# Attention scores of one layer as products over 64 rows, one softmax map on each half of the TensorE array

## The chip, the cores and the metric

The kernel runs on one core of a Trainium2 chip. The metric is the device time of one execution in microseconds (us). The kernel before takes 610.21 us, the median of three runs (609.72 to 611.18).

The engines are called by the profile's short names: PE is TensorE's matmul, PEld the loading of its stationary operand, DVE is VectorE, ACT is ScalarE, POOL is GpSimd, and SP is the engine that issues most of the DMAs. PSUM is the memory that PE writes, in banks of 128 partitions by 512 numbers.

## The reference

One decoder layer on 512 tokens of width 1024, in float32. One projection makes nine groups of columns. Branch A is a gated MLP over chunks of 128 tokens; branch B is differential attention with 8 heads; both are projected, gated, merged and projected again, and a LayerNorm ends the layer. What the change touches is the scores of branch B:

```python
q = apply_rope(qh.reshape(bn, s_len, B_HEADS, 2, B_QK_DIM), cos, sin) * (B_QK_DIM ** -0.5)
k = apply_rope(kh.reshape(bn, s_len, B_HEADS, 2, B_QK_DIM), cos, sin)
...
sc = jnp.einsum("bqhmd,bkhmd->bhmqk", qblk, k, preferred_element_type=jnp.float32)
sc = jnp.where(mask, sc, -jnp.inf)
pr = jax.nn.softmax(sc, axis=-1)
a = pr[:, :, 0] - lam * pr[:, :, 1]
return jnp.einsum("bhqk,bkhd->bqhd", a.astype(v.dtype), v)
```

Each of the 8 heads has two softmax maps (m = 0 and 1), and each map has queries and keys of 64 numbers (`B_QK_DIM`, in the kernel `DK`). The queries are taken 128 at a time, so a head has four blocks, and block i looks at (i + 1) * 128 keys: 128, 256, 384 or 512.

## The kernel before

**Products.** PE multiplies a stationary operand (128 rows by 128 columns, loaded first) with a moving one (128 rows by up to 512 columns); the sum runs over the rows, that is over SBUF's partitions. The operands are of the type float32r, which keeps fewer bits than float32. So a float32 number is kept as two parts, high (its rounding to float32r) and low (the rest), and a product is made of several. For the large projections `three` (line 279) makes three: high by high, high by low, low by high.

**Order of the work.** The whole program is one list of instructions in a written order. `product` (line 267) issues a product of the projections and counts it. `later(n, fn)` (line 262) puts a piece of other work on an agenda, to be issued n products later. So the attention runs between the products of other projections: `attention` (line 871) gives each of the 32 blocks (8 heads by 4) a starting count, some 13 to 23 products apart (`PERIOD`, for the last two heads times 0.78). At a block's start `scores` is issued, 10 to 13 products later `combine`, at the start of the block two further on `transposes`, and one further on `values`. Only the products of `product` are counted: those of the scores, the transposes and the values are not, so the agenda does not move when their number changes.

**Rotary and stacks.** `rope` (line 694) handles a pair of heads (p = 0 to 3) for q or k. Two feature groups of the projection come out as two banks, A with the first half of the rotated numbers and B with the second. DVE makes the rotated halves (`turn`, `join`), ACT rounds them to their high parts (`high`, line 707), POOL subtracts to get the low parts (`low`, line 712). The four planes are kept in one tile `hl`, 128 partitions by 4 planes by 512 tokens, in the order high of half 0, high of half 1, low of half 1, low of half 0. A partition of `hl` is one of 32 frequencies times four (two heads by two maps).

`get` (line 720), 14 or 18 products after `low`, then makes the **stacks** with DMAs on SP's queue: for each head and map the 32 partitions by 4 planes are laid out as 128 partitions. A stack tile is 128 partitions by 2 maps by 512 tokens. So all 128 rows of one map's product carry the 64 numbers twice, as high and as low parts. For k there is a second stack `kx` with the planes in reversed order, so that its high parts lie opposite the low parts of q. For the first pair (p = 0) `kx` is made much later from `k` by `change_over` (line 735, 290 products on, `SWAP`), with four DMAs of 32 partitions for each head, because the buffers that `kx` has (the tag "kx") hold sums of weights at first (line 941).

**Scores.** `scores` (line 763) makes, for one block of one head, two products for each map: q by k (high by high and low by low, in one sum over 128 rows) and q by kx (high by low and low by high). Each map writes its own PSUM bank (`ps_sc`, two buffers). DVE then adds the mask and takes the smallest value (line 776), and ACT takes the exponential (line 782).

Of the kernel before, what the change touches and what calls it, by code (L numbers as in the profile page):

```python
# [13 lines left out]
F32 = mybir.dt.float32  # L14
F32R = mybir.dt.float32r
BF16 = mybir.dt.bfloat16
I32 = mybir.dt.int32
AF = mybir.ActivationFunctionType
# [3 lines left out]
P = 128  # L22
D = 1024
T = 512
# [3 lines left out]
DK = 64  # L28
# [15 lines left out]
ROPE_Q = (2, 6, 8, 20, 22)  # L44
STACK = (14, 4)
FIRST_STACK = (20, 4)
SWAP = 290
BEGIN = 14
STRETCH = 0.78
PERIOD = (13, 16, 20, 23)  # L50
# [183 lines left out]
def hybrid_layer(ctx: ExitStack, tc: tile.TileContext, a, out: bass.AP):  # L234
    nc = tc.nc
    pe, dve, act, pool, sp = nc.tensor, nc.vector, nc.scalar, nc.gpsimd, nc.sync
# [9 lines left out]
    def pbank(tag, bufs):  # L246
        return psum.tile([P, T], F32, tag=tag, name=f"ps_{tag}", bufs=bufs)

    def pp():
        return pbank("pp", 3)  # L250
# [11 lines left out]
    def later(n, fn, *args):  # L262

        clock[1] += 1
        heapq.heappush(agenda, (clock[0] + n, clock[1], fn, args))
# [132 lines left out]
    def next_unit(name):  # L398
        u = cursor[0]
        assert STEPS[u][0] == name, (STEPS[u][0], name)  # L400
        cursor[0] += 1
        for g in (prep(u), prep(u + 1), prep(u + 2)):
            run(g)
        if not pumping:
            for v in range(u + 3, u + 6):
                run(load(v))
        spread(u + 3)
        if name in EARLY_ASK:
            later(ASK, lambda: run(load(u + 6)))
        return split.pop(u)  # L410
# [31 lines left out]
    def feature_group(ps, name, mh, ml):  # L442
        h, l = next_unit(name)
        for k in range(KT):
            s = slice(k * P, (k + 1) * P)
            three(ps, h[:, s], l[:, s], mh[:, k, :], ml[:, k, :], k == 0, k == KT - 1)
# [36 lines left out]
    ap_ = attn.enter_context(tc.tile_pool(name="attn", bufs=1))  # L483
# [23 lines left out]
    def small(shape, name, bufs=6):  # L507
        return consts.tile(shape, F32, name=name, tag=name, bufs=bufs)
# [183 lines left out]
    stacks = {}  # L692

    def rope(name, p, banks=None, at=None, stack=STACK):

        A, B = banks or (pp(), pp())
        m, parts = [], []

        def turn(bank, table):
            m.append(rp.tile([P, T], F32, name="m", tag="m", bufs=6))  # L700
            dve.tensor_tensor(out=m[-1], in0=bank, in1=table, op=OP.mult)

        def join():
            dve.tensor_tensor(out=m[0], in0=m[0], in1=m[3], op=OP.subtract)
            dve.tensor_tensor(out=m[2], in0=m[2], in1=m[1], op=OP.add)

        def high():
            parts.append(rp.tile([P, 4, T], F32R, name="hl", tag="hl"))
            for j in range(2):
                act.activation(parts[0][:, j, :], m[2 * j], AF.Copy)  # L710

        def low():
            hl = parts[0]
            for j in range(2):
                pool.tensor_tensor(out=hl[:, 3 - j, :], in0=m[2 * j], in1=hl[:, j, :].bitcast(F32),  # L715
                                   op=OP.subtract)
            for hd in range(2):
                later(stack[0] + stack[1] * hd, get, hd)

        def get(hd):  # L720


            h = 2 * p + hd
            for n in ("k", "kx") if name == "k" and p else (name,):
                s = ap_.tile([P, 2, T], F32R, name=n, tag=n, bufs=3)
                stacks[n, h] = s
                for i in range(2):
                    rows = parts[0][2 * hd + i:P:4]
                    if n == "kx":
                        rows = rows[:, ::-1]  # L730
                    sp.dma_start(out=s[:, i, :].bitcast(F32), in_=rows.bitcast(F32))
            if name == "k" and p == 0:
                later(SWAP + 6 * hd, change_over, h)

        def change_over(h):
            s = ap_.tile([P, 2, T], F32R, name="kx", tag="kx", bufs=3)
            stacks["kx", h] = s
            for b in range(4):
                sp.dma_start(out=s[b:P:4].bitcast(F32), in_=stacks["k", h][3 - b:P:4].bitcast(F32))

        at = at or ROPE[:2] + (ROPE if name == "k" else ROPE_Q)
        for i, bank in enumerate((A, B)):
            if not banks:
                feature_group(bank, name, xh, xl)
            later(at[2 * i], turn, bank, cs)
            later(at[2 * i + 1], turn, bank, sn)
        for n, fn in zip(at[4:], (join, high, low)):
            later(n, fn)
# [13 lines left out]

    def scores(h, i):
        n = (i + 1) * P
        q, k0, k1 = stacks["q", h], stacks["k", h], stacks["kx", h]
        sc = [pbank("sc", 2) for _ in range(2)]
        for m in range(2):
            for o, kk in enumerate((k0, k1)):
                pe.matmul(sc[m][:, :n], q[:, m, i * P:(i + 1) * P], kk[:, m, :n],  # L769
                          start=o == 0, stop=o == 1)  # L770
        pr = [ap_.tile([P, T], F32, name=f"p{m}", tag=f"p{m}", bufs=3) for m in range(2)]
        if i == 0:
            todo["st", h] = small([P, NT, 4], "sth", 2)
        st = todo["st", h][:, i, :]
        for m in range(2):
            dve.tensor_tensor_reduce(out=pr[m][:, :n], in0=sc[m][:, :n], in1=mask[:, T - n:],  # L776
                                     scale=-(DK ** -0.5), scalar=3e38, op0=OP.add, op1=OP.min,
                                     accum_out=st[:, m:m + 1])
            if m == 0:
                dve.tensor_scalar(out=st[:, 0:1], in0=st[:, 0:1], scalar1=-math.log(T),  # L780
                                  scalar2=None, op0=OP.add)
            act.activation(pr[m][:, :n], pr[m][:, :n], AF.Exp, bias=st[:, m:m + 1], scale=-1.0,  # L782
                           accum_out=st[:, 2 + m:3 + m])
        todo[h, i] = pr, st
# [75 lines left out]
    def block(h, i, starts):  # L860
        e = NT * h + i
        later(starts[e], scores, h, i)
        later(starts[e] + COMBINE[i], combine, h, i)
        later(starts[e + 2], transposes, h, i)
        later(starts[e + 3], values, h, i)
        if i == NT - 1:
            tail = TAIL if h < 5 else LAST_TAIL
            for d, fn in zip(tail, (squares, norm, scale, gated)):
                later(starts[e + 3] + d, fn, h)
# [76 lines left out]
    for k in range(KT):  # L946
        if k % 2 == 0:
            h, l = next_unit("kq")
        s = [slice((k % 2) * T + i * P, (k % 2) * T + (i + 1) * P) for i in range(4)]
# [6 lines left out]
        else:  # L956
            for i, bank in enumerate(first_kq):
                three(bank, h[:, s[i]], l[:, s[i]], xh[:, k, :], xl[:, k, :], False, k == KT - 1)
    rope("k", 0, first_kq[:2], TURN_K, FIRST_STACK)
    rope("q", 0, first_kq[2:], TURN_Q, STACK)  # L960
    first_ua = ua_pair(0, (pbank("tr", 1), pbank("po", 1)))

# [23 lines left out]
    for p in range(1, 4):  # L986
        rope("k", p)
        rope("q", p)
        later(GATE, ua_pair(p, (pp(), pp())))
# [273 lines left out]
    for c in (1, 0):  # L1263
        h, l = next_unit("ple")
        for t in range(NT):
            ts = slice(t * P, (t + 1) * P)
            for k in range(2):
                m = slice(k * T, (k + 1) * T)
# [103 lines left out]
    for those in ((0, 1), (2, 3)):  # L1372
        for k in range(KT):
# [9 lines left out]
            h, l = units[k // 2]  # L1383
            m = slice((k % 2) * T, (k % 2 + 1) * T)
# [9 lines left out]
    for t in range(NT):  # L1394
        ts = slice(t * P, (t + 1) * P)
        for i, (c0, c1) in enumerate(last_columns[t][1:], 1):
            for k in range(KT):
# [4 lines left out]
                h, l = units[k // 2]  # L1402
                m = slice((k % 2) * T + c0 - T, (k % 2) * T + c1 - T)
# [45 lines left out]
```

## Time and profile before

| What | Value |
|---|---|
| median of three runs | 610.21 us |
| the profiled execution, its own time | 610.13 us |
| its span, first to last instruction | 608.2 us |
| PE busy | 600.1 us (99%), 2880 products |
| weight loads (PEld) | 503.1 us (83%) |
| DVE, ACT, POOL busy | 464.8, 346.7, 125.4 us |
| mean granted TensorE clock | 0.997 of full speed |
| data moved by DMA | 138.23 MB, mean 227 GB/s |
| products of the scores (line 769) | 128, between 117.0 and 283.6 us |

A row of the profile names the line of the kernel, the engine, the operation, and what it writes and reads, out<-in, by the program's names, then the shapes and the count. "128*128" is the number of active rows and columns of the array, and "128x512" the moving operand. The ends of products are modelled, and products overlap in the array; so it is the distance from one product's start to the next one's start that tells what a product costs in a dense stretch. A few records are missing.

### The profile page before, as it was taken

How to read it: one execution, taken by the hardware profiler on the slowest of the kernel's cores; microseconds unless marked ns; L12 is line 12 of the kernel's file. 1: busy time of each engine (PE TensorE's matmuls, PEld its weight loads, DVE VectorE, ACT ScalarE, POOL GpSimd, SP SyncE). 2: the span in 40 equal slices, each digit the busy share in tenths (PEclk: the TensorE clock that was granted, in tenths of full speed). 3: DMA queues.
4: the chain of work that ended last, by engine and by line, in shares of the span. 5: the costliest groups of instructions: out<-in, count | busy, mean ns of one | idle time of the engine just before them, and what ended most of it. 6: DMA issues, size and time to landing. Idle time of an engine off the chain costs nothing.

```text
span 608.2 us, 8270 instructions
## 1 busy us (share of the span) xinstructions
PE 600.1 (99%) x2880; PEld 503.1 (83%) x2880; DVE 464.8 (76%) x770; ACT 346.7 (57%) x537; POOL 125.4 (21%) x133
## 2 busy tenths in 40 slices
PE   9999999999999999999999999999999999999995
PEld 6888888888888888888888888888888888888885
DVE  6995645588789789678965788779687887879476
ACT  6656475755745745746676666554776565555310
POOL 1234121041252432422110321331120011110011
PEclk9999999999999999999999999999999999999998
DMA  8689899697887896892579988976999578997002
GB/s 309 228 246 182 252 205 227 237 240 252 277 208 277 273 258 230 240 313 61 150 310 288 305 241 217 273 175 191 286 244 306 172 206 250 253 256 288 27 35 103
DMA packets 44541, 138.23 MB, mean 227 GB/s; under 512 B 5940, under 2 KB 7092, under 8 KB 44148
## 3 DMA queue, kind: packets, MB, share of 16 engines
q1 hardware_dynamic: 34436, 102.97, 46.8%
q0 software_dynamic: 9488, 34.35, 30.6%
q8 instruction: 22, 0.36, 0.2%
q10 hardware_dynamic: 576, 0.39, 0.2%
q14 instruction: 19, 0.16, 0.1%
HBM read 118.69 MB, written 29.49 MB: 244 GB/s over the span
## 4 chain that ended last, share of the span: by engine, by line
PE 98%; DVE 1%; DMA 0%; DVEq 0%; issue 0%
PE ps_pp L268 56%; PE ps_sc L268 22%; PE ps_tx L268 9%; PE ps_sc L769 3%; PE ps_po L814 3%; PE ps_tr L803 1%; PE ps_po L268 1%; PE ps_tr L268 1%; PE ps_tr L1133 1%; PE ps_po L1133 1%; PE ps_tx L857 1%; DMA xr<-in_xT 0%; PE ps_po L1319 0%; PE ps_tr L1319 0%; DVE base L1361 0%; DVE xl L295 0%
## 5 line engine op out<-in xcount | busy, mean ns | idle before, releaser
L392 DVE TENSOR_TENSOR wl<-wr,wh 128x1024 fp32r<-128x1024 f32 x133 | 165.4, 1250 | 36.7 <-ACT wh L389 36.5
L389 ACT ACTIVATE wh<-wr 128x1024 fp32r<-128x1024 f32 x133 | 139.4, 1054 | 68.7 <-PE ps_pp L268 20.5
L268 PE MATMUL ps_pp<-xh,wh 128*128 128x512 f32 x232 | 91.2, 394 | 0.0
L268 PE MATMUL ps_pp<-xh,wl 128*128 128x512 f32 x232 | 91.0, 393 | 0.0
L268 PE MATMUL ps_pp<-xl,wh 128*128 128x512 f32 x232 | 90.4, 391 | 0.1
L365 POOL DMA_DIRECT2D wr<-in_w x30 | 25.8, 872 | 153.6 <-DVE wl L392 150.6
L268 PE MATMUL ps_pp<-wl,xh 128*128 128x512 f32 (+1 forms) x148 | 56.9, 384 | 0.0
L268 PE MATMUL ps_pp<-wh,xl 128*128 128x512 f32 (+1 forms) x148 | 56.8, 384 | 0.0
L268 PE MATMUL ps_pp<-wh,xh 128*128 128x512 f32 (+1 forms) x148 | 56.7, 383 | 0.0
L782 ACT ACTIVATE p<-p,sth 128x128 f32<-128x128 f32 (+3 forms) x64 | 35.5, 556 | 28.2 <-DVE sth L780 28.0
L268 PEld LDWEIGHTS ps_pp<-xl,wh 128*128 128x128 f32 x232 | 43.6, 188 | 9.3 <-DVE xl L295 0.5
L268 PEld LDWEIGHTS ps_pp<-xh,wh 128*128 128x128 f32 x232 | 43.5, 188 | 9.0 <-ACT wh L294 0.6
L268 PEld LDWEIGHTS ps_pp<-xh,wl 128*128 128x128 f32 x232 | 43.6, 188 | 8.7
L776 DVE CUSTOM_DVE_ANT_0 p<-ps_sc,mask 128x128 f32<-128x128 f32 (+3 forms) x64 | 31.0, 484 | 19.3 <-PE ps_sc L769 19.1
L268 PE MATMUL ps_sc<-wl,xsh 128*128 128x512 f32 x88 | 34.5, 392 | 0.0
L268 PE MATMUL ps_sc<-wh,xsh 128*128 128x512 f32 x88 | 34.4, 390 | 0.0
L268 PE MATMUL ps_sc<-wh,xsl 128*128 128x512 f32 x88 | 34.3, 390 | 0.0
L805 ACT ACTIVATE at<-ps_tr 128x128 f32<-128x128 f32 (+3 forms) x32 | 13.9, 436 | 32.9 <-PE ps_tr L803 27.5
L715 POOL TENSOR_TENSOR hl<-m,hl 128x512 fp32r<-128x512 f32 x16 | 23.4, 1502 | 43.9 <-ACT hl L710 26.6
L268 PEld LDWEIGHTS ps_pp<-wl,xh 128*128 128x128 f32 x148 | 27.8, 188 | 5.4
L268 PEld LDWEIGHTS ps_pp<-wh,xh 128*128 128x128 f32 x148 | 27.8, 188 | 5.4
L268 PEld LDWEIGHTS ps_pp<-wh,xl 128*128 128x128 f32 x148 | 27.8, 188 | 5.4
(304 smaller groups left out, 1335.2 us busy)
## 6 DMA issues: line engine op xcount, KB each, us to landing
wr<-in_w SPq DMA_DIRECT2D x83, 512.0 KB, 5.2
wr<-in_w POOLq DMA_DIRECT2D x30, 512.0 KB, 6.7
wa<-in_w POOLq DMA_DIRECT2D x12, 512.0 KB, 6.2
k<-hl SPq DMA_DIRECT2D x16, 256.0 KB, 4.8
q<-hl SPq DMA_DIRECT2D x16, 256.0 KB, 3.9
ws_va<-in_w POOLq DMA_DIRECT2D x8, 512.0 KB, 9.8
wr<-ws_va SPq DMA_DIRECT2D x8, 512.0 KB, 4.7
kx<-hl SPq DMA_DIRECT2D x12, 256.0 KB, 4.5
```

The lines of the kernel that those rows point to most:

```text
L268: pe.matmul(ps, s, m, start=start, stop=stop, skip_group_check=read_within)
L365: pool.dma_start(out=raw[u], in_=weights(STEPS[FOLLOWS[u]][1]), accum_op=OP.add)
L389: act.activation(h, raw[u], AF.Copy)
L392: dve.tensor_tensor(out=l, in0=raw[u], in1=h.bitcast(F32), op=OP.subtract)
L715: pool.tensor_tensor(out=hl[:, 3 - j, :], in0=m[2 * j], in1=hl[:, j, :].bitcast(F32), op=OP.subtract)
L769: pe.matmul(sc[m][:, :n], q[:, m, i * P:(i + 1) * P], kk[:, m, :n], start=o == 0, stop=o == 1)
L776: dve.tensor_tensor_reduce(out=pr[m][:, :n], in0=sc[m][:, :n], in1=mask[:, T - n:], scale=-(DK ** -0.5), scalar=3e38, op0=OP.add, op1=OP.m ...
L782: act.activation(pr[m][:, :n], pr[m][:, :n], AF.Exp, bias=st[:, m:m + 1], scale=-1.0, accum_out=st[:, 2 + m:3 + m])
L803: pe.transpose(tr[:, j * P:(j + 1) * P], ad[:, j * P:(j + 1) * P], ident)
L805: act.activation(at[:, :n], tr[:, :n], AF.Copy)
L814: pe.matmul(po[:, i * P:(i + 1) * P], at[:, j * P:(j + 1) * P], v[:, j, h * P:(h + 1) * P], start=j == 0, stop=j == i)
L1133: pe.matmul(sa[:, t * P:(t + 1) * P], va[:, t, g * P:(g + 1) * P], aux[0][:, 0, g, :], start=True, stop=True)
```

## The change

The order of the planes in `hl` becomes high of half 0, low of half 0, high of half 1, low of half 1. A stack tile has the same size as before, but map 0 lies on partitions 0 to 63 and map 1 on partitions 64 to 127, and its second dimension holds the two parts, high and low, where it held the maps. Each of the two DMAs of a stack now writes 64 partitions, each with the two parts of 512 tokens in one piece (4 KB), where it wrote 128 partitions with one piece of 2 KB. The stacks `kx`, their DMAs and `change_over` are gone. The buffers of the tag "kx" stay, for the other tiles that use them.

`scores` now issues six products where it issued four, each over 64 rows: high by high for map 0 (upper half of the array) and for map 1 (lower half), then low of q by high of k for both, then high of q by low of k for both. Low by low is left out. Each map still sums into its own bank.

```diff
         def high():
...
-                act.activation(parts[0][:, j, :], m[2 * j], AF.Copy)
+                act.activation(parts[0][:, 2 * j, :], m[2 * j], AF.Copy)
...
-                pool.tensor_tensor(out=hl[:, 3 - j, :], in0=m[2 * j], in1=hl[:, j, :].bitcast(F32),
+                pool.tensor_tensor(out=hl[:, 2 * j + 1, :], in0=m[2 * j], in1=hl[:, 2 * j, :].bitcast(F32),
...
-            for n in ("k", "kx") if name == "k" and p else (name,):
-                s = ap_.tile([P, 2, T], F32R, name=n, tag=n, bufs=3)
-                stacks[n, h] = s
-                for i in range(2):
-                    rows = parts[0][2 * hd + i:P:4]
-                    if n == "kx":
-                        rows = rows[:, ::-1]
-                    sp.dma_start(out=s[:, i, :].bitcast(F32), in_=rows.bitcast(F32))
-            if name == "k" and p == 0:
-                later(SWAP + 6 * hd, change_over, h)
-
-        def change_over(h):
-            s = ap_.tile([P, 2, T], F32R, name="kx", tag="kx", bufs=3)
-            stacks["kx", h] = s
-            for b in range(4):
-                sp.dma_start(out=s[b:P:4].bitcast(F32), in_=stacks["k", h][3 - b:P:4].bitcast(F32))
+            s = ap_.tile([P, 2, T], F32R, name=name, tag=name, bufs=3)
+            stacks[name, h] = s
+            for i in range(2):
+                rows = parts[0][2 * hd + i:P:4]
+                sp.dma_start(out=s[i * DK:(i + 1) * DK].bitcast(F32), in_=rows.bitcast(F32))
...
     def scores(h, i):
         n = (i + 1) * P
-        q, k0, k1 = stacks["q", h], stacks["k", h], stacks["kx", h]
+        q, k = stacks["q", h], stacks["k", h]
         sc = [pbank("sc", 2) for _ in range(2)]
-        for m in range(2):
-            for o, kk in enumerate((k0, k1)):
-                pe.matmul(sc[m][:, :n], q[:, m, i * P:(i + 1) * P], kk[:, m, :n],
-                          start=o == 0, stop=o == 1)
+        for o, (qp, kp) in enumerate(((0, 0), (1, 0), (0, 1))):
+            for m in range(2):
+                rows = slice(m * DK, (m + 1) * DK)
+                pe.matmul(sc[m][:, :n], q[rows, qp, i * P:(i + 1) * P], k[rows, kp, :n], start=o == 0, stop=o == 2)
```

More of the change, by code (lines that the diff above doesn't have):

```diff
@@ L46 @@
 FIRST_STACK = (20, 4)
-SWAP = 290
 BEGIN = 14
```

## The prediction

> **What bounds the kernel now.** I read the page first: the busy times, the granted clock, and the chain of waits that ended last.
>
> ```profile
> span 608.2 us, 8270 instructions
> ...
> PE 600.1 (99%) x2880; PEld 503.1 (83%) x2880; DVE 464.8 (76%) x770; ACT 346.7 (57%) x537; POOL 125.4 (21%) x133
> ...
> PEclk9999999999999999999999999999999999999998
> ...
> PE 98%; DVE 1%; DMA 0%; DVEq 0%; issue 0%
> PE ps_pp L268 56%; PE ps_sc L268 22%; PE ps_tx L268 9%; PE ps_sc L769 3%; PE ps_po L814 3%; PE ps_tr L803 1%; PE ps_po L268 1%; PE ps_tr L268 1%; PE ps_tr L1133 1%; PE ps_po L1133 1%; PE ps_tx L857 1%; DMA xr<-in_xT 0%; PE ps_po L1319 0%; PE ps_tr L1319 0%; DVE base L1361 0%; DVE xl L295 0%
> ```
>
> 98% of the chain is PE at full clock, so the time is the sum of what the products cost, one behind the other. The scores (line 769) are 3% of it. Whatever the change adds to or takes from PE's queue in the stage of the scores therefore moves the end by as much; whatever it takes from SP, POOL or the DMAs moves nothing by itself. The instructions of line 769:
>
> ```profile
> L769 PE MATMUL ps_sc<-k,q x64: 220/336/474, 117.0 to 283.4; 128*128 128x128 f32 x16, 128*128 128x256 f32 x16, 128*128 128x384 f32 x16, 128*128 128x512 f32 x16
> L769 PE MATMUL ps_sc<-kx,q x64: 273/308/398, 117.1 to 283.6; 128*128 128x128 f32 x16, 128*128 128x256 f32 x16, 128*128 128x384 f32 x16, 128*128 128x512 f32 x16
> ```
>
> There are 128 products, 32 of each width, four to a block. Their durations (0.22 to 0.47 us) overlap, so I price them by the distance from start to start, in the timeline of PE for one block of each width. The columns are the start, the duration and the instruction. I leave out the first product of each block, whose start is disturbed by the transposes ahead of it.
>
> ```profile
> 205.13 0.28 PE L769 MATMUL ps_sc<-kx,q 128*128 128x128 f32 x1
> 205.24 0.28 PE L769 MATMUL ps_sc<-k,q 128*128 128x128 f32 x1
> 205.35 0.27 PE L769 MATMUL ps_sc<-kx,q 128*128 128x128 f32 x1
> 205.46 0.45 PE L268 MATMUL ps_pp<-xh,wl 128*128 128x512 f32 x1
> ...
> 209.71 0.28 PE L769 MATMUL ps_sc<-kx,q 128*128 128x256 f32 x1
> 209.83 0.28 PE L769 MATMUL ps_sc<-k,q 128*128 128x256 f32 x1
> 209.95 0.28 PE L769 MATMUL ps_sc<-kx,q 128*128 128x256 f32 x1
> 210.07 0.60 PE L857 MATMUL ps_tx<-ident,on 128*128 128x128 f32 x4
> ...
> 215.34 0.34 PE L769 MATMUL ps_sc<-kx,q 128*128 128x384 f32 x1
> 215.51 0.34 PE L769 MATMUL ps_sc<-k,q 128*128 128x384 f32 x1
> 215.69 0.33 PE L769 MATMUL ps_sc<-kx,q 128*128 128x384 f32 x1
> 215.86 0.39 PE L268 MATMUL ps_pp<-xl,wh 128*128 128x512 f32 x1
> ...
> 221.10 0.39 PE L769 MATMUL ps_sc<-kx,q 128*128 128x512 f32 x1
> 221.33 0.39 PE L769 MATMUL ps_sc<-k,q 128*128 128x512 f32 x1
> 221.56 0.40 PE L769 MATMUL ps_sc<-kx,q 128*128 128x512 f32 x1
> 221.79 0.39 PE L268 MATMUL ps_pp<-xh,wh 128*128 128x512 f32 x1
> ```
>
> From the first to the fourth row of each group are three steps: 0.33, 0.36, 0.52 and 0.69 us, so a step is 0.11, 0.12, 0.173 and 0.23 us for 128, 256, 384 and 512 keys. One step of each width is 0.633 us; four steps and 8 heads make 0.633 x 4 x 8 = **20.3 us** for all scores. The narrowest two widths cost almost the same: something other than the moving columns binds there. The timeline of the weight loads around the first of these blocks shows what:
>
> ```profile
> 204.85 0.14 PEld L803 LDWEIGHTS ps_tr<-ident,p 128*128 128x128 f32 x1
> 204.96 0.19 PEld L769 LDWEIGHTS ps_sc<-k,q 128*128 128x128 f32 x1
> 205.07 0.19 PEld L769 LDWEIGHTS ps_sc<-kx,q 128*128 128x128 f32 x1
> 205.18 0.19 PEld L769 LDWEIGHTS ps_sc<-k,q 128*128 128x128 f32 x1
> 205.29 0.19 PEld L769 LDWEIGHTS ps_sc<-kx,q 128*128 128x128 f32 x1
> 205.40 0.19 PEld L268 LDWEIGHTS ps_pp<-xh,wl 128*128 128x128 f32 x1
> ```
>
> A load starts every 0.11 us though each is recorded as 0.19 us long, so two are under way at a time, and each starts before the product ahead of it has ended. From transposes to scores to a projection the 0.11 us goes on: these changes of kind cost nothing. But all of them use the whole array (128*128).
>
> **The change, part by part.**
>
> *The pairs.* Six products over 64 rows replace four over 128. If map 0 and map 1 run beside each other, a block takes three steps: 0.633 x 3 x 8 = 15.2 us, which saves 20.3 - 15.2 = **5.1 us**. No row shows two products beside each other, so I bound it. At the one end lies this saving. At the other they run one after the other in six steps: 0.633 x 6 x 8 = 30.4 us, 10.1 us more than before. Between them, the streams run side by side but the six loads follow each other at 0.11 us: 0.66 us for each of the three narrow blocks and 3 x 0.23 = 0.69 us for the widest, so (3 x 0.66 + 0.69) x 8 = 21.4 us, 1.1 us more than before. I take the saving of 5.1 us: the two maps share no partition of the operands and no PSUM bank, and the rows above show two loads under way at once even where they share all 128 rows.
>
> The Trainium skill, "TensorE: Matmul & The Clock Gate", Part 3 (Measured speedup vs the span model), gives 3.07 times for four products of 32 rows side by side, not 4. If two got the same 77%, six products would cost what 3.9 steps cost, an estimate from that page that would leave hardly any gain; no run here shows it yet.
>
> *The change of grouping.* Each of the 32 blocks now stands between products of 128 rows, so the array goes from 128 rows to two times 64 and back: 64 changes. The trace has none. At the lower end a change costs nothing, as between the three kinds of product above. At the upper end the array has to be empty before the next load begins: a product of 512 columns is recorded as 0.39 us where the next one starts after 0.23 us, so 0.16 us of it is still under way then, and the load of 0.19 us would come behind that: 0.35 us, 64 times, 22.4 us. Between them the array empties while the load already runs, as every load above runs under a product: 0.16 us, 64 x 0.16 = **10.2 us**. I take this one. A product over 128 rows must be summed over both halves, and a pair must not be; the trace shows that a product is still under way for 0.16 us when the next begins, and two groupings at once in the same columns seem the less likely thing to me.
>
> The Trainium skill, "TensorEngine Tiling (Array Packing)", section Tiling Modes, says that a change of the tiling mode, other than a change of tile within it, drains the engine. It gives no price, and no row of before can confirm it.
>
> *The stacks and their DMAs.* Here SP's queue and the landings matter:
>
> ```profile
> kx<-hl SPq DMA_DIRECT2D x12, 256.0 KB, 4.5
> kx<-k SPq DMA_DIRECT2D x8, 128.0 KB, 3.8
> ...
> DMA to landing us min/median/max: 2.3/3.9/4.1
> ...
> 153.12 1.18 SPq L731 DMA_DIRECT2D q<-hl  x2
> ...
> 159.50 0.19 PEld L769 LDWEIGHTS ps_sc<-k,q 128*128 128x128 f32 x1
> ```
>
> The 12 and the 8 DMAs go, 4.2 MB and some 20 issues, and with them what they held up on SP's queue. PE waits for none of the transfers behind them (DMA has 0% of the chain), so this is worth 0. The cover is thinnest for q: for head 2 its two DMAs are issued from 153.12 on, the second at about 153.7, and land at 157.8 by the longest landing of q (4.1 us, the third row); the first load of that head's scores is at 159.50. So 1.7 us are spare. The new transfers write half the partitions in pieces twice as long. `kx` from `k`, whose pieces have that length on a quarter of the partitions, takes 3.8 us for half the bytes. At the lower end the landing stays at 3.9 us and costs nothing; at the upper end it doubles, is 2.4 us late, and this at the first head of the three later pairs: 7 us. I take 0, as the row nearest in the length of its pieces lands in the same time.
>
> *Behind the scores.* Map 0's bank is now complete with the fifth product of six, not the second of four: in a wide block some 0.2 us later. DVE comes later than that in any case:
>
> ```profile
> 154.60 0.68 DVE L776 CUSTOM_DVE_ANT_0 p<-ps_sc,mask 128x512 f32<-128x512 f32 x1
> ...
> DVE p L776 <- PE ps_sc L769: 19.1, 15, 2.3
> ```
>
> The block that started at 152.61 is read only from 154.60 on. Where DVE does wait (19.1 us in all) it is idle anyway, and PE wants the result only two blocks later. The high and low parts are the same work on other planes: 0.
>
> **The sum.** -5.1 (three steps for four) + 10.2 (64 changes of grouping) + 0 (DMAs) + 0 (DVE) = +5.1 us. The profiled execution took 610.13 us, 1.9 us around its span of 608.2, and lies at the median of the runs (610.21). So **615.3 us**, 0.8% slower.
>
> **The rivals.**
>
> *The changes of grouping cost little or nothing.* Then the three steps are what counts: 610.2 - 5.1 = 605.1 us, the other side. For it: 0.11 us from load to load right through three kinds of product, and loads that start ahead in the queue. Against: none of these alters which rows are summed. It decides from 5.1 / 64 = 0.08 us a change; below that the kernel is faster.
>
> *The array empties and the load comes only then.* 64 x 0.35 - 5.1 = +17.3, so 627.5 us. For it: a load for half the rows belongs to the new grouping too. Against: loads go ahead of running products everywhere in the trace.
>
> *The halves do not run beside each other* (the change doesn't do what it says): six steps, +10.1, so 620.3 us, if the changes are free. Against: separate partitions and banks.
>
> *The loads follow one another.* +1.1, so 611.3 us with free changes. For it: 0.11 us is the smallest distance between two loads of 128 columns in the rows above. Against: none of those had rows to itself.
>
> **How the numbers follow.** Chances: my forecast (0.16 us a change, or near it) 0.38; cheap changes 0.34; emptying and load 0.12; not side by side 0.08; loads in a row 0.08. A difference under 0.2%, 1.2 us, can hardly be told from no change here. Faster are the cheap changes, 0.34. The loads in a row lie at the bound: most of them, 0.06, count as the same. The rest, 0.60, is slower. The range reaches from 604.5 (the cheap changes with 0.6 us to spare) to 624 (a change of 0.30 us, or no running side by side), and leaves out the dearest changes. As cases of both signs hold much of it: the forecast alone lies between 612 and 620 (0.11 to 0.23 us a change).
>
> **What would show it.** In PE's timeline of after, products of 64 rows should start in pairs, a few ns apart; starts 0.11 us apart or more within a pair say that loads or halves follow one another. The step from the last product ahead of a block to its first pair, and from its last pair to the next full product, should hold 0.16 us more than a plain step each; if not, the rival of cheap changes holds, and if 0.35, the next one. PE's busy time does not show this, for its ends are modelled. The wait rows should show no PE waiting on `q` or `k`; if they do, the landings were what I had wrong. My forecast is wrong if a change costs under 0.08 us, or if blocks of 512 keys take other than three steps between the changes.

## The result and the profile after

The kernel after takes **617.59 us** (median of four runs, 617.40 to 617.74), the kernel before 610.61 us (four runs, 609.72 to 611.18). The ratio is 1.0116, with a 95% interval from 1.0098 to 1.0133: 7.0 us slower. The profiled execution of after took 617.54 us.

The lines of the page of after that answer those shown of before:

```profile
span 615.8 us, 8362 instructions
...
PE 607.2 (99%) x2944; PEld 498.9 (81%) x2944; DVE 465.1 (76%) x770; ACT 346.5 (56%) x537; POOL 125.6 (20%) x133
...
PE 98%; DMA 1%; DVE 0%; DVEq 0%; ACT 0%; issue 0%; ACTq 0%
```

PE still makes 98% of the chain. It has 64 products more and its loads are busy for 4 us less, and it takes longer. To see where, I cut both executions at the last product before the first block of scores and at the last transpose of the last head. The columns of this view are the stretch, its length, the busy time (and count) of PE, PEld, DVE, ACT and POOL, the granted clock, and the DMAs. First the kernel before:

```profile
0.00:116.80 116.80, 115.42 (x501) 93.67 (x502) 79.38 (x109) 72.33 (x93) 23.83 (x35) 1.00 0.84 229
116.80:292.20 175.40, 175.40 (x942) 151.52 (x941) 142.19 (x377) 105.30 (x231) 53.56 (x51) 1.00 0.80 242
292.20:608.20 316.00, 309.24 (x1440) 257.90 (x1438) 243.23 (x284) 169.04 (x215) 48.00 (x47) 1.00 0.74 218
```

The same of the kernel after:

```profile
0.00:117.30 117.30, 115.61 (x502) 93.67 (x502) 79.40 (x109) 72.23 (x93) 23.83 (x35) 1.00 0.86 220
117.30:299.60 182.30, 182.30 (x1006) 147.24 (x1005) 142.57 (x377) 105.20 (x231) 53.52 (x51) 1.00 0.83 216
299.60:615.80 316.20, 309.26 (x1440) 257.97 (x1438) 243.08 (x284) 169.05 (x215) 48.26 (x47) 0.99 0.75 218
```

The stage of the scores is 182.3 - 175.4 = 6.9 us longer, which is the whole of the 7.0 us. The stretch after it is the same, and the half microsecond ahead of it comes from a wait at the very start, which varies: in the traces of the experiments below the first scores start between 117.0 and 118.0 us. In the stage the clock is 1.00 in both.

One block of 512 keys of head 4, in the timeline of after (the start, the time, the engine and instruction, how many of a kind, and in brackets the idle time of that engine):

```profile
225.35 0.38 PE L791 MATMUL ps_tr<-ident,p 128*128 128x128 f32 x2
...
225.66 0.53 PEld L758 LDWEIGHTS ps_sc<-k,q 64*128 64x128 f32 x6 [0.17 <-issue]
225.66 0.96 PE L758 MATMUL ps_sc<-k,q 64*128 64x512 f32 x6
...
226.55 0.19 PEld L267 LDWEIGHTS ps_pp<-xh,wh 128*128 128x128 f32 x1 [0.36 <-issue]
226.56 0.50 PE L267 MATMUL ps_pp<-xh,wh 128*128 128x512 f32 x1
226.66 0.19 PEld L267 LDWEIGHTS ps_pp<-xl,wh 128*128 128x128 f32 x1
226.89 0.40 PE L267 MATMUL ps_pp<-xl,wh 128*128 128x512 f32 x1
```

The timeline merges like instructions; PE's timeline of three short stretches inside the same block takes the six apart:

```profile
225.66 0.50 PE L758 MATMUL ps_sc<-k,q 64*128 64x512 f32 x2
...
226.00 0.39 PE L758 MATMUL ps_sc<-k,q 64*128 64x512 f32 x2
...
226.23 0.40 PE L758 MATMUL ps_sc<-k,q 64*128 64x512 f32 x2
```

Six products make three pairs, and the plain step from the second to the third is 0.23 us: the pairs run as one product did. But the steps next to a change of grouping are longer. Into the block, the first pair starts 0.31 us after the first of the two transposes, where two plain steps of 0.11 make 0.22, and the second pair 0.34 after the first, where a plain step is 0.23. Out of it, the next product starts 0.33 us after the third pair, and the one behind it another 0.33 us later. So a change costs about 0.1 us twice. The loads say why: the first load of the new grouping does not run ahead as all loads of before did. It starts at 226.55, with its product. The third pair started at 226.23 and by the plain step streams for 0.23 us, to 226.46, so nothing streams for 0.09 us; and the next product's plain spacing only begins one load's distance (0.11 us, 226.55 to 226.66) later. **Emptying 0.09, a load that nothing covers 0.11: 0.20 us a change** beside wide products. (That the array empties in the 0.09 us is a reading; what the rows show is that the load starts only then.) In the narrow blocks, where the loads bind anyway, some of it is hidden. The block of 128 keys of the same head, in PE's timeline of after, cut in the same way (the row x4 is the second and the third pair together):

```profile
208.99 0.27 PE L791 MATMUL ps_tr<-ident,p 128*128 128x128 f32 x1
209.19 0.33 PE L758 MATMUL ps_sc<-k,q 64*128 64x128 f32 x2
209.35 0.39 PE L758 MATMUL ps_sc<-k,q 64*128 64x128 f32 x4
209.46 0.27 PE L758 MATMUL ps_sc<-k,q 64*128 64x128 f32 x2
```

The first pair again starts 0.09 us later than the plain step of 0.11 after the last transpose, but the second pair only 0.05 us later than that step after the first. The third pair follows the second by 0.11 us, the plain step: the two loads of a pair do not follow one another.

The mean comes from the stage: it lost 6.9 us although three steps in place of four were to save 5.1, so 64 changes cost 12.0 us, 0.19 us each.

### The profile page after: what moved, and what is told of

Read it like the earlier page. It is cut to its first block, busy times and chain, and to the rows that moved or that the text cites. A ratio compares the mean times of both kernels' runs of the same rounds, so it can differ in the third digit from the quotient of the medians.

```text
span 615.8 us, 8362 instructions
## 1 busy us (share of the span) xinstructions
PE 607.2 (99%) x2944; PEld 498.9 (81%) x2944; DVE 465.1 (76%) x770; ACT 346.5 (56%) x537; POOL 125.6 (20%) x133
## 4 chain that ended last, share of the span: by engine, by line
PE 98%; DMA 1%; DVE 0%; DVEq 0%; ACT 0%; issue 0%; ACTq 0%
PE ps_pp L267 56%; PE ps_sc L267 21%; PE ps_tx L267 9%; PE ps_sc L758 3%; PE ps_po L802 3%; PE ps_tr L791 1%; PE ps_po L267 1%; PE ps_tr L267 1%; DMA wr<-in_w 1%; PE ps_tx L845 1%; PE ps_tr L1121 1%; PE ps_po L1121 1%; PE ps_tr L1307 0%; PE ps_po L1307 0%; DVE base L1349 0%; DVEq L1433 0%
```

## The experiments

The theory: the pairs are worth the step they save, and the 64 changes of grouping cost 12 us. The rivals: the cost is in the pairs (their loads, or that they do not run beside each other), or in the new stacks.

**Three full products a block.** The stacks and their DMAs as after the change, no grouping:

```diff
-        sc = [pbank("sc", 2) for _ in range(2)]
+        sc = [pbank("sc", 2)] * 2
         for o, (qp, kp) in enumerate(((0, 0), (1, 0), (0, 1))):
-            for m in range(2):
-                rows = slice(m * DK, (m + 1) * DK)
-                pe.matmul(sc[m][:, :n], q[rows, qp, i * P:(i + 1) * P], k[rows, kp, :n], start=o == 0, stop=o == 2)
+            pe.matmul(sc[0][:, :n], q[:, qp, i * P:(i + 1) * P], k[:, kp, :n], start=o == 0, stop=o == 2)
```

> The stacks and DMAs of the change stay, but a block of scores is three products over all 128 rows into one bank, in place of three pairs over 64 rows into two. Each product then sums both maps, and both maps read that sum: the scores are not those of the reference, only their time counts. There is no change of grouping. Theory (the 64 changes of grouping cost some 12 us and the three steps save 5.1): 610.6 - 5.1 = 605.5 us. Rival (the new stacks, whose DMAs land after 6.2 us where it was 3.9 and 4.8, hold the work up): it stays at 617.6 us.

Measured: 606.29 us, ratio 0.9931 (0.9916 to 0.9946) to the 610.41 us of before: 4.1 us faster. Without changes of grouping the steps do save, and the stacks do not cost 7 us. But 1.0 us of the 5.1 is missing. PEld's timeline of this kernel shows where most of it goes, here at the first block of head 4:

```profile
203.09 0.19 PEld L756 LDWEIGHTS ps_sc<-k,q 128*128 128x128 f32 x1 [0.26 <-issue]
```

The rows of tile q for that head's two DMAs (issue duration and time, and the time to landing, each as min/median/max or first to last):

```profile
L727 SPq DMA_DIRECT2D q<-hl x2: 572/586/600, 197.0 to 197.6; - x2
...
DMA to landing us min/median/max: 4.2/4.8/5.4
```

And in the list of waits (in total, times, longest):

```profile
PEld ps_sc L756 <- issue: 0.7, 3, 0.3
```

The second DMA, issued at 197.6, lands 5.4 us later, at 203.0, and the load starts right behind it, after an idle 0.26 us. This happens three times, 0.7 us in all. The new stacks land later than those of before (2.4 to 2.5 us there, see below), and in a shorter stage that is too late.

The two kernels also give the price of a change without the assumed saving: they have the same stacks and the same three steps a block, so what after takes longer is the changes. From the first of the two transposes to the second product behind the block, the block of 512 keys of head 4 took 1.54 us in after (225.35 to 226.89). In PE's timeline of this kernel:

```profile
218.41 0.38 PE L789 MATMUL ps_tr<-ident,p 128*128 128x128 f32 x2
218.55 0.93 PE L756 MATMUL ps_sc<-k,q 128*128 128x512 f32 x3
219.32 0.40 PE L267 MATMUL ps_pp<-xh,wh 128*128 128x512 f32 x1
219.56 0.39 PE L267 MATMUL ps_pp<-xl,wh 128*128 128x512 f32 x1
```

Here it is 1.15 us: 0.39 us for two changes, 0.20 each. The medians agree: 617.59 - 606.29 = 11.3 us, and with the 0.7 us of late stacks, which after does not have, 12.0 us for 64 changes.

**More changes, the same pairs.** The third pair is issued one projection product later:

```diff
+        pairs_of(((0, 0, 0), (1, 1, 0)))
+        later(1, scores_end, h, i, sc, pairs_of)
+
+    def scores_end(h, i, sc, pairs_of):
+        n = (i + 1) * P
+        pairs_of(((2, 0, 1),))
```

> The change, with the third pair of each block one projection product later than the first two: the same pairs, but four changes of grouping a block in place of two. Theory (a change costs 0.19 us, as the stage of the scores took 6.9 us more and the steps were to save 5.1, so 12.0 over 64): 64 x 0.19 = 12.2 us more, 629.8 us. Rival (what costs is in the pairs themselves, their loads above all): the same number of pairs, 617.6 us.

Measured: 630.47 us, 1.0326 (1.0310 to 1.0341), 12.9 us more than after. The same pairs, twice the changes, twice the cost: 12.9 / 64 = 0.20 us a change. The rival in which the cost belongs to the pairs falls.

**Fewer changes, the same pairs.** Blocks 0 and 1 of a head share their banks:

```diff
+        if i != 1:
+            todo["sc"] = [pbank("sc", 2) for _ in range(2)]
+            for e, c in ((0, 0), (1, P)) if i == 0 else ((i, 0),):
...
+                        pe.matmul(todo["sc"][m][:, c:c + (e + 1) * P], q[rows, qp, e * P:(e + 1) * P],
+                                  k[rows, kp, :(e + 1) * P], start=o == 0, stop=o == 2)
```

> The change, with the products of blocks 0 and 1 of a head issued together (128 and 256 columns side by side in the same banks): the same pairs, 48 changes of grouping in place of 64. Theory: 16 x 0.19 = 3.0 us less, 614.6 us. Rival (the cost is in the pairs): 617.6 us.

Measured: 615.19 us, 1.0077 (1.0062 to 1.0092), 2.4 us less than after. The sign and most of the size are the theory's: 2.4 / 16 = 0.15 us a change. The two changes that this takes away lie beside the narrowest blocks, where a change is cheaper.

**One map after the other.**

```diff
-        for o, (qp, kp) in enumerate(((0, 0), (1, 0), (0, 1))):
-            for m in range(2):
+        for m in range(2):
+            for o, (qp, kp) in enumerate(((0, 0), (1, 0), (0, 1))):
                 rows = slice(m * DK, (m + 1) * DK)
```

> The change, with the three products of map 0 first and then those of map 1, so that only the third and the fourth can run beside each other: five steps a block in place of three, as many changes of grouping. If halves do run beside each other and this is worth a whole step: 2 x 0.633 x 8 = 10.1 us more, 627.7 us. If they do not, and the gain never was there: 617.6 us.

Measured: 617.46 us, 1.0118 (1.0101 to 1.0135): nothing changes. That is the number that I had put down to halves that do not run beside each other. The block of 512 keys says otherwise; PE's timeline of this kernel:

```profile
225.31 0.97 PE L758 MATMUL ps_sc<-k,q 64*128 64x512 f32 x6
```

All six products take 0.97 us, as in after (0.96), and three shorter stretches show that they start in three pairs here too:

```profile
225.31 0.51 PE L758 MATMUL ps_sc<-k,q 64*128 64x512 f32 x2
225.65 0.40 PE L758 MATMUL ps_sc<-k,q 64*128 64x512 f32 x2
225.88 0.40 PE L758 MATMUL ps_sc<-k,q 64*128 64x512 f32 x2
```

The records do not name the half. But the next run shows that products on one half start 0.23 us apart, so a pair must be one product of each map: map 1's first product, written behind all three of map 0, did not wait for them. So this run did not test what I meant it to test, and showed something else: see the last section. What running side by side is worth needed a run in which it cannot happen:

```diff
-                rows = slice(m * DK, (m + 1) * DK)
+                rows = slice(0, DK)
```

> The change, with the products of both maps on the upper 64 rows (both read map 0's half of the stacks, so map 1's scores are those of map 0; only the time counts): no two products can run beside each other, the changes of grouping are as many. In the run with one map after the other the starts lay 10 ns apart in pairs all the same, so the question is open what the running side by side is worth. If it is worth a whole step a pair: six steps a block in place of three, 3 x 0.633 x 8 = 15.2 us more, 632.8 us. Rival (the array takes one product at a time anyway, and the close starts in the trace are only those of the queue): 617.6 us.

Measured: 632.23 us, 1.0366 (1.0347 to 1.0384), 14.6 us more than after, where a whole step a pair is 15.2. The same block in PE's timeline:

```profile
208.26 1.66 PE L758 MATMUL ps_sc<-k,q 64*128 64x512 f32 x6
```

1.66 us for the same six products against 0.96: three more steps of 0.23. The two halves do run at full speed beside each other.

**A change of grouping by itself.** Two kernels with the stacks, the DMAs and the four products of before, and one product more ahead of each block, once over 64 rows and once, as the control, over 128:

```diff
+        pe.matmul(sc[0][:128, :P], q[:64, 0, i * P:i * P + 128], k0[:64, 0, :P], start=True, stop=True)
         for m in range(2):
             for o, kk in enumerate((k0, k1)):
```

> The kernel before, with one more product of 64 rows and 128 columns ahead of each block's four (upper half, into map 0's bank, overwritten by the block's own first product). Stacks, DMAs and the block's products are those of before; only the changes of grouping are new, 64 of them. Theory (0.19 us a change): 64 x 0.19 = 12.2, and 32 steps of 0.11 = 3.5, so 610.6 + 15.7 = 626.3 us. Rival (the cost is in the pairs or in the stacks): only the steps, 614.1 us.

> The kernel before, with one more product of 128 rows and 128 columns ahead of each block's four: the control, without a change of grouping. All theories: 32 x 0.11 = 3.5 us more, 614.1 us.

Measured: 624.73 us with 64 rows, 1.0237 (1.0223 to 1.0251), and 614.13 us with 128, 1.0063 (1.0050 to 1.0075), against 610.39 us for before. The control is what was expected. The difference between the two is 10.6 us for 64 changes: 0.17 us each, a little under the 0.19 expected. So the cost comes with the grouping alone, in the old kernel too. A third kernel has a narrower stationary operand for the same product (`[:66, :P]` and `i * P + 66`):

> As the product of 64 rows ahead of each block, but with a stationary operand of 66 columns in place of 128, so that its load is about half as long (0.05 us less). If a load after a change of grouping starts only when the array is empty, the time falls by 32 x 0.05 = 1.7 us against the one with 128 columns. If the load runs while the array empties, the two are the same.

Measured: 623.45 us, 1.0222 (1.0208 to 1.0236), 1.3 us less. The intervals overlap, so the times alone do not decide. The timelines of a block of 512 keys do. With 128 columns:

```profile
205.05 0.32 PE L767 MATMUL ps_sc<-k,q 64*128 64x128 f32 x1
...
205.30 0.19 PEld L770 LDWEIGHTS ps_sc<-k,q 128*128 128x128 f32 x1
```

With 66 columns:

```profile
204.45 0.27 PE L767 MATMUL ps_sc<-k,q 64*66 64x128 f32 x1
...
204.65 0.19 PEld L770 LDWEIGHTS ps_sc<-k,q 128*128 128x128 f32 x1
```

From the product of 64 rows to the next load it is 0.25 us in the one and 0.20 in the other: the 0.05 us by which the load is shorter are saved on the path. So a load behind a change of grouping is not hidden by the emptying. A sooner emptying behind the narrower operand would look the same in this pair of runs; the other ground for the uncovered load is the step behind the first wide product of a new grouping, which is longer by 0.10 us.

**The stacks in four pieces.** Each of the two DMAs of a stack is cut in two, one for each part:

```diff
-                sp.dma_start(out=s[i * DK:(i + 1) * DK].bitcast(F32), in_=rows.bitcast(F32))
+                for part in range(2):
+                    sp.dma_start(out=s[i * DK:(i + 1) * DK, part].bitcast(F32), in_=rows[:, part::2].bitcast(F32))
```

> The change, with each stack written by four DMAs of 128 KB (64 partitions, pieces of 2 KB as before the change) in place of two of 256 KB with pieces of 4 KB. If the pieces' length made the landings of q longer (second DMA of a head's stack: 2.5 us before, 5.4 after, at heads 4 and 6), they go back towards 2.5 us; if it is that only 64 partitions are written, the last of the four lands no sooner than some 5 us after its issue. The time stays near 617.6 us if PE does not wait for the stacks.

Measured: 617.84 us in a single run, too close to 617.59 to tell a difference. The landings of q for head 4, by kernel; before:

```profile
L731 SPq DMA_DIRECT2D q<-hl x2: 572/584/597, 198.6 to 199.2; - x2
...
DMA to landing us min/median/max: 2.4/2.4/2.5
```

after:

```profile
L727 SPq DMA_DIRECT2D q<-hl x2: 573/582/592, 202.6 to 203.2; - x2
...
DMA to landing us min/median/max: 4.2/4.8/5.4
```

and in four pieces:

```profile
L728 SPq DMA_DIRECT2D q<-hl x4: 563/581/591, 200.4 to 204.1; - x4
...
DMA to landing us min/median/max: 2.7/2.9/3.4
```

With pieces of 2 KB they land almost as before, on 64 partitions too (the landing of the fourth is not on record here; at head 6 all four take 2.6 to 3.0 us). So at these heads it was how the DMA is cut, not the number of partitions. Whether the length of a piece or the size of a DMA counts isn't told apart. Nor is it the whole: over all heads the landings of q have a median of 3.9 us before, 6.2 after and 4.3 in four pieces, and the longest are 4.1, 8.8 and 8.4 us.

None of this points to a valid kernel that beats the one before. By the measured prices, the two changes of a group must be shared by more than 12.0 / 5.1 = 2.4 blocks before they pay, and the two PSUM banks of the scores hold 512 columns of each map, mostly one block or two.

## Why the prediction was right or wrong

It gave 615.3 us and slower; measured were 617.6 us and slower. The bound it started from, that only PE's queue in the stage of the scores counts, held: the other two stretches did not move. Of the 2.3 us between forecast and result, 1.8 are in the price of the changes (12.0 us in place of 10.2), and 0.4 in the kernel before, whose median is 610.61 us over the four runs beside after's, where the forecast started from 610.21.

**The pairs: right.** A saving of 5.1 us was taken. Putting both maps on one half costs 14.6 of the 15.2 us worked out the same way, and three full products save 4.1 us, with 0.7 us lost to late stacks. The doubt put beside it from the Trainium skill, "TensorE: Matmul & The Clock Gate", Part 3 (3.07 times for four), is not what two halves do here: the pairs lose nothing to speak of.

**The change of grouping: right in kind, wrong in its parts.** The step was that the array empties for 0.16 us while the load already runs, 10.2 us in all. Measured were 0.19 us and 12.0 us, from the stage, and 0.15, 0.17 and 0.20 us in three experiments. But the parts are those of the rival that I gave 0.12: the load comes only when the array is empty. That rival's price of 0.35 us was too high, because both of its terms were recorded durations. The recorded end of a product suggested 0.16 us of emptying where it is 0.09, and the recorded load of 0.19 us takes 0.11 us of the queue's time, as its distance from the next load had shown all along. The two mistakes, a hidden load and an emptying that was too long, nearly cancelled: that the price came out so close was luck. My ground for the hidden load, that every load of before ran under a product, did not carry over to a load of another grouping.

The page of the Trainium skill that was cited for this, "TensorEngine Tiling (Array Packing)", section Tiling Modes, says that a change of mode drains the engine. The trace agrees, with 0.09 us; that the next load has to wait for it as well, which is the larger part, is not in that sentence.

**The DMAs: right in the sum, wrong in the reason.** I took the landings to be unchanged, and the second DMA of a head's q went from 2.5 to 5.4 us at head 4 and from 2.5 to 5.9 at head 2. The row I had gone by, `kx` from `k` with 3.8 us, moved half the bytes, and did not carry over. At head 2, for which I had counted on 1.7 us to spare, the two DMAs of after and the first load of that head's scores are:

```profile
L727 SPq DMA_DIRECT2D q<-hl x2: 536/567/598, 155.4 to 156.0; - x2
...
DMA to landing us min/median/max: 4.2/5.1/5.9
...
162.04 0.30 PEld L758 LDWEIGHTS ps_sc<-k,q 64*128 64x128 f32 x4 [0.17 <-issue]
```

Issued at 156.0, landed at 161.9, loaded at 162.04: 0.1 us was left, which is no more than what lies between landing and load where the load does wait (203.0 to 203.09 with three full products). The idle 0.17 us is that of the change, as at other heads. At head 4 the stack landed at 208.6 and the first load came at 209.19, so 0.6 us were left:

```profile
209.19 0.41 PEld L758 LDWEIGHTS ps_sc<-k,q 64*128 64x128 f32 x6 [0.17 <-issue]
```

So the DMAs cost nothing in after, but by a narrow margin, and because the stage itself had become longer: head 2's load comes 6.0 us after the issue, where it was 5.8 in before (153.7 to 159.50). In the faster run with three full products nothing was left. This 0 was partly luck too.

**Behind the scores: right.** DVE waits longer for the scores than the 19.1 us of before, as the list of waits of after has it, and nothing waits for that on PE:

```profile
DVE p L764 <- PE ps_sc L758: 27.2, 19, 2.6
```

**The rivals.** Cheap changes (0.34) are out: they would have had to cost under 0.08 us. Loads that follow one another are out, since the pairs of the narrow blocks go at the plain step of 0.11 us. Halves that do not run together are out by the run with both maps on one half.

## What to carry to other kernels

Products over the two halves of the array's rows run beside each other at full speed, but going into and out of that grouping empties the array and leaves the next load uncovered: here 0.2 us each time, nearly a 512-column product. So group them in long runs; in a dense stream of full products a handful of half products loses more than it saves. And price such a step by the distance between starts, for loads as for products, not by recorded durations.

## What the runs showed of the hardware that was not expected

The two halves of the array need not keep to one common order. With map 0's three products written ahead of map 1's, the six took 0.97 us as against 0.96 us in alternating order, and started in the same three pairs. The Trainium skill, "TensorE: Matmul & The Clock Gate", Part 3 (What overlaps and what doesn't), has products start and end strictly in program order; for products on different halves this run does not agree, if the products reached PE in the order in which the kernel writes them, which the records do not show.

A DMA of 256 KB between SBUF tiles landed after 4.2 to 5.4 us in pieces of 4 KB on 64 partitions, and after 2.4 to 2.5 us in pieces of 2 KB on 128, at the same place of the kernel (q of head 4); in four DMAs of 128 KB, in pieces of 2 KB on 64 partitions, three of the four landed after 2.7 to 3.4 us.
